# Feed-forward block: weights as the moving operand for gate and up, and 32x32 blocks turned on VectorE

## The chip, the cores and the metric

The kernel runs on one core of a Trainium2 chip. The metric is device time in microseconds (us): the median over three timed executions. Beside them there is one execution recorded by the hardware profiler; all durations below come from that one.

## The reference

A trunk of four pre-norm residual layers on 256 tokens of width 1024, all in float32. Layers 0 and 3 mix tokens with sparse attention (NSA), layer 1 with block attention (MoBA), layer 2 with a short gated convolution. Each layer then applies a dense SwiGLU feed-forward block, and a last RMSNorm ends the trunk. What the change touches is the feed-forward block:

```python
def swiglu(a, w_gate, w_up, w_down):
    return (jax.nn.silu(a @ w_gate) * (a @ w_up)) @ w_down

a = rms_norm(h, norm_ffn[i])                      # h: 256 x 1024
h = h + swiglu(a, ffn_w_gate[i], ffn_w_up[i], ffn_w_down[i])   # D_FF = 2816
```

Per layer that is gate and up, 1024 x 2816 each, and down, 2816 x 1024.

## The kernel before

**Layout.** Activations are kept transposed: features on the 128 partitions, the 256 tokens along the free axis. The residual is eight tiles of 128 x 256 (`self.h`). 2816 features are 22 tiles (`FT`), 1024 are 8 (`KT`).

**Float32 from two parts.** Each operand x is held as a high part (rounded to the type fp32r) and a low part x - high. A product is the sum of three matmuls: high by high, high by low, low by high. Activations are split into a tile of shape [128, 2, 256]: index 0 is high, index 1 is low (`split`, L175: the copy on ScalarE, the subtraction on VectorE).

**Weights.** All weights of the program lie in device memory as one stream of 128x128 tiles in the order of use, cut into parts of 8 tiles (512 KB). `load_part` (L84) issues one transfer of a part from the SP queue into one of 4 `raw` buffers. `split_part` (L91) makes the high part (ScalarE, L109) and the low part (VectorE, L110) into one of 5 `whi` and 5 `wlo` buffers. `take` (L113) hands out tiles in order; when it enters part q it has emitted the load and the split of all parts up to q + 4. A `raw` buffer comes free when its split is done, a `whi`/`wlo` pair when TensorE has used the part. So the transfer of part q + 8 can be issued when part q + 4 is split, and that can be done when TensorE has left part q - 1.

**Matmul.** In `group_wide` (L132) the weight tile is the stationary operand (128x128, loaded ahead of each matmul), and the activations move. With the high weight the high and low activations move as one block of 512 columns and land side by side in one PSUM bank; with the low weight the 256 high activations move:

```python
mm(outs[o], w[0], acts[k].rearrange("p i s -> p (i s)"), ...)   # 512 columns
mm(outs[o][:, :S], w[1], acts[k][:, 0, :], ...)                 # 256 columns
```

That is two matmuls per weight tile, 16 in a part.

**Feed-forward block** (`ffn`, L288). First f = 0 and 1 together (four banks), then one f at a time: eight tiles of gate, eight of up, then `act`. For each f `act` adds the two halves of a bank (`half`: copy on ScalarE L294, add on VectorE L295), scales by the row of reciprocal norms `rb` while f < 7 (L297), applies Silu (L303), multiplies by up (L305), and splits the product into an `ff` tile (L177, L178). From f = 7 on the operand is the normed activation (`normed`, L278), made beside f = 2 to 5. The norm's sums over features (`rms_sums`, L219) are four small matmuls ahead of the last tiles of the first group; `rms_tokens` makes the reciprocal per token (VectorE, GpSimd), `rms_rows` (L234) turns it into rows.

**Down** (`out_proj`, L261) uses `group_wide` with the 22 `ff` tiles: first four output tiles together, feature tile by feature tile (11 parts), then four output tiles one by one.

**Another order that the program already has.** `values` (L338), in the attention layers, has the activations stationary and the weights moving: for each of 8 feature tiles and each half of the tokens, three matmuls of 512 columns, tokens on the partitions of the result:

```python
mm(p, a[:, 0, s], ws[k][0], ...)   # L348
mm(p, a[:, 0, s], ws[k][1], ...)   # L349
mm(p, a[:, 1, s], ws[k][0], ...)   # L350
```

**Order of the work.** The program is written in the order above; a scheduler of the language sets waits and buffers and may interleave what is independent. Every engine and the SP queue then run their own lists in order. PSUM has eight banks, in rings A (4), B (3) and C (1).

Of the kernel before, what the change touches and what calls it, by code (L numbers as in the profile page):

```python
# [10 lines left out]
F32R = mybir.dt.float32r  # L11
AF = mybir.ActivationFunctionType
OP = mybir.AluOpType
# [3 lines left out]
P = 128  # L17
D = 1024
S = 256
KT = D // P  # L20
NT = S // P
DFF = 2816
FT = DFF // P
# [4 lines left out]
PART = 8  # L28
# [2 lines left out]
RAW_BUFS = 4  # L31
W_BUFS = 5
PR_BUFS = 4
FF_BUFS = 24
ROW_BUFS = 7
PT_BUFS = 5
# [15 lines left out]
class Kernel:  # L52
    def __init__(self, ctx, tc, ap):
        self.tc, self.nc, self.ap = tc, tc.nc, ap
        self.const = ctx.enter_context(tc.tile_pool(name="const", bufs=1))
        self.wp = ctx.enter_context(tc.tile_pool(name="wp", bufs=3))
        self.work = ctx.enter_context(tc.tile_pool(name="work", bufs=2))
        self.ps = ctx.enter_context(tc.tile_pool(name="ps", bufs=2, space=PSUM))
        self.pos = 0
        self.raw = {}  # L60
        self.parts = {}
        self.nblk = ap["w"].shape[0]
        self.names = [step for step, name, _, c in stream()
                      for _ in range(len(c) // P * (FT if name == "ffn_w_down" else 4 if step == "F" else KT))][::PART]
        self.n = 0
# [8 lines left out]
    def ff(self, shape, dt=F32R):  # L74
        return self.work.tile(shape, dt, tag="ff", name=self.uid("ff"), bufs=FF_BUFS)

# [7 lines left out]
    def load_part(self, q, cut=1):  # L84
        t = self.wp.tile([P, PART * P], F32, tag="raw", name=f"raw{q}", bufs=RAW_BUFS)
        n = PART * P // cut
        for i in range(cut):
            self.nc.sync.dma_start(t[:, i * n:(i + 1) * n], self.ap["w"][q, :, i * n:(i + 1) * n])
        self.raw[q] = t

    def split_part(self, q):  # L91
# [21 lines left out]
    def take(self, n=1):  # L113

        q, o = divmod(self.pos, PART)
        assert o + n <= PART
        for x in range(q, min(q + AHEAD, self.nblk)):
            if x not in self.parts:
                self.split_part(x)
        self.pos += n  # L120
        hi, lo = self.parts[q]
        return hi[:, o * P:(o + n) * P], lo[:, o * P:(o + n) * P]
# [52 lines left out]
    def split(self, dst, src):  # L175

        self.nc.scalar.copy(dst[:, 0], src)  # L177
        self.nc.vector.tensor_tensor(out=dst[:, 1], in0=src, in1=dst[:, 0].bitcast(F32), op=OP.subtract)  # L178
# [39 lines left out]

    def rms_sums(self):  # L219
        nc = self.nc  # L220
        pt = self.sums = self.bank("C" if self.norm == 8 else "B")
        for t in range(NT):
            c = slice(t * P, (t + 1) * P)
            nc.tensor.matmul(pt[:, t:t + 1], self.ssq[:, c], self.ones, start=True, stop=False)
            nc.tensor.matmul(pt[:, t:t + 1], self.sq[:, c], self.ones, start=False, stop=True)
# [49 lines left out]
            m += n  # L275


    def normed(self, k, norm):  # L278

        nc = self.nc  # L280
        if k % 2 == 0:
            self.pair = self.sb([P, 2, 2, S], "pt", F32R, bufs=PT_BUFS)
        a, x = self.pair[:, k % 2], self.row()
        nc.vector.scalar_tensor_tensor(x, self.h[k], self.gain[:, norm, k:k + 1], self.rb, op0=OP.mult, op1=OP.mult)
        self.split(a, x)
        return a

    def ffn(self, norm):  # L288
        nc = self.nc
        hs, at, final = [], self.begin(norm), []  # L290

        def half(dst, p, scale):

            nc.scalar.copy(dst, p[:, S:])  # L294
            nc.vector.tensor_tensor(out=dst, in0=p[:, :S], in1=dst, op=OP.add)  # L295
            if scale:
                nc.vector.tensor_tensor(out=dst, in0=dst, in1=self.rb, op=OP.mult)  # L297

        def act(pg, pu, scale):
            gu = self.sb([P, 2, S], "gu")  # L300
            sg, hf = self.row(), self.row()
            half(gu[:, 0, :], pg, scale)
            nc.scalar.activation(sg, gu[:, 0, :], AF.Silu)  # L303
            half(gu[:, 1, :], pu, scale)
            nc.vector.tensor_tensor(out=hf, in0=sg, in1=gu[:, 1, :], op=OP.mult)  # L305
            h2 = self.ff([P, 2, S])
            self.split(h2, hf)
            hs.append(h2)

        def products(f, a):  # L310
            p = [self.bank(c) for c in ("AA", "CB", "AA", "AA", "BB")[f - 2 if f < 4 else 2 + f % 3]]
            for o in p:
                self.group_wide([o], a)
            return p

        ps = [self.bank(c) for c in "AABB"]
        self.group_wide(ps, at)
        self.rms_tokens()
        p = products(2, at)
        self.rms_rows()  # L320
        for f in range(2):
            act(ps[2 * f], ps[2 * f + 1], True)
        for f in range(2, FT):
            late = f < 7
            if f > 2:
                p = products(f, at if late else final)
            act(*p, late)
            if len(final) < KT:
                final += [self.normed(len(final) + i, norm) for i in range(2)]
        self.out_proj(hs, norm + 1)  # L330


# [23 lines left out]
    def softmax(self, cols, gates):  # L356

        nc = self.nc
        pr = self.sb([P, 3 * S], "pr", bufs=PR_BUFS)
        mn = self.sb([P, 4], "mn", bufs=3)  # L360
# [496 lines left out]
def wide_tiles(w, cols):  # L857

    k, n = w.shape[0] // P, len(cols) // P
    return w[:, cols].reshape(k, P, n, P).transpose(0, 2, 1, 3).reshape(k * n, P, P)  # L860


def stream():

    r = lambda a, n: np.arange(a, a + n)
    out = lambda w, j, step: [(step, w, j, r(0, 512))] + [(step, w, j, r(m * P, P)) for m in range(4, KT)]
    s = []
    for i in LAYERS:
        j = i // 3
        n = {}  # L870
        if i % 3 == 0:
            for step in NSA_ORDER:
                k = step[0]
                n[k] = m = int(step[1:]) if step[1:] else n.get(k, -1) + 1
                cols = {"A": r(1024, 512), "K": r(1536 + m // 2 * 512 + m % 2 * P, P), "G": r(2480, P),
                        "V": np.concatenate([r(1792, 256), r(2304, 256)]), "q": r(m * P, P)}.get(k)
                if k == "F":
                    s.append((k, "nsa_cmp_w1", j, r(m * 512, 512)))
                elif cols is not None:
                    s.append((k, "nsa_w_in", j, cols))  # L880
            s += out("nsa_w_out", j, "nsa_out")
        elif i % 3 == 1:
            for step in MOBA_ORDER:
                k = step[0]
                n[k] = m = int(step[1:]) if step[1:] else n.get(k, -1) + 1
                cols = {"V": r(2048 + m * 512, 512), "k": r(1024 + m * P, P), "q": r(m * P, P)}.get(k)
                if cols is not None:
                    s.append(("moba_" + k, "moba_w_in", j, cols))
            s += out("moba_w_out", j, "moba_out")
        else:  # L890
            s.append(("conv", "conv_w_in", j, np.concatenate([r(b, P) for b in (1024, 2048, 0)])))
            for c in range(1, KT):
                s += [("conv", "conv_w_in", j, r(b + c * P, P)) for b in (1024, 2048, 0)]
            s += out("conv_w_out", j, "conv_out")
        s.append(("ffn", "ffn_gate_up", i, np.concatenate([r(c, P) for c in (0, DFF, P, DFF + P)])))
        for f in range(2, FT):
            s += [("ffn", "ffn_gate_up", i, r(b + f * P, P)) for b in (0, DFF)]
        s += out("ffn_w_down", i, "down")
    return s


def tiles(x):

    x = dict(x)
    x["ffn_gate_up"] = np.concatenate([x["ffn_w_gate"], x["ffn_w_up"]], axis=2)
    x["nsa_cmp_w1"] = np.concatenate([x["nsa_cmp_k_w1"], x["nsa_cmp_v_w1"]], axis=2)
    ts = []
    for step, name, j, c in stream():
        w = x[name][j]
        ts.append(wide_tiles(w[c], np.arange(512)) if step == "F" else wide_tiles(w, c))  # L910
    t = np.concatenate(ts)
    assert t.shape[0] % PART == 0
    return np.ascontiguousarray(t.reshape(-1, PART, P, P).transpose(0, 2, 1, 3)).reshape(-1, P, PART * P)
# [41 lines left out]
```

## Time and profile before

| | us |
|---|---|
| three timed executions | 1301.71, 1302.19 (median), 1303.94 |
| the profiled execution's own time | 1303.46 |
| its span, first to last instruction | 1301.7 |
| TensorE busy in the span | 1259.3 |
| VectorE busy | 981.8 |
| ScalarE busy | 717.2 |
| GpSimd busy | 309.1 |

The span is 1.76 us shorter than the execution's own time. Busy times of an engine are from start to end of its instructions; a matmul's end is modelled, and matmuls overlap, so the distance between the starts of two matmuls tells what one costs. The mean granted TensorE clock is 0.992 of full speed. DMA moved 215.24 MB.

### The profile page before, as it was taken

The page shows a single profiled execution, that of the slowest core. Times are in us where ns is not written, and L with a number is a line of the kernel's source. Part 1 is how long each engine was busy: PE and PEld are TensorE (multiplying, and loading weights), DVE is VectorE, ACT ScalarE, POOL GpSimd, SP SyncE. Part 2 cuts the span into 40 slices and gives each one's busy share as a digit, 9 for nine tenths or more (in the row PEclk, how much of TensorE's full clock was granted, in tenths as well). Part 3 has the DMA queues.
Part 4 walks back from the last instruction along what each step waited for, and adds up shares of the span by engine and source line. Part 5 has one row for each costly group of instructions (what it writes and reads, how often), then busy time and mean ns, then how long its engine had stood idle before and what let it go on. Part 6 is the DMA issues. An engine that isn't in the chain of part 4 may idle for free.

```text
span 1301.7 us, 21379 instructions
## 1 busy us (share of the span) xinstructions
PE 1259.3 (97%) x7820; PEld 1122.1 (86%) x7820; DVE 981.8 (75%) x1947; ACT 717.2 (55%) x1445; POOL 309.1 (24%) x336
## 2 busy tenths in 40 slices
PE   8888999999998999999999999999998989999997
PEld 8877788888888888888899988888898778888886
DVE  7588799775778888876667789775767797996753
ACT  5469757554335546655434357554324796666532
POOL 2467610000356320000113120000334765000011
PEclk9999999999999999999999999999999999999999
DMA  8623065656554335655555655656555312566551
GB/s 275 234 72 100 33 195 177 196 193 193 181 178 131 108 119 178 211 193 194 168 191 177 194 179 173 200 188 196 182 178 195 98 49 73 187 210 192 186 180 57
DMA packets 60728, 215.24 MB, mean 165 GB/s; under 512 B 7248, under 2 KB 7632, under 8 KB 60624
## 3 DMA queue, kind: packets, MB, share of 16 engines
q1 hardware_dynamic: 60480, 213.85, 50.5%
q8 instruction: 61, 1.00, 0.3%
q14 instruction: 43, 0.35, 0.1%
q10 hardware_dynamic: 144, 0.04, 0.0%
HBM read 212.81 MB, written 1.05 MB: 164 GB/s over the span
## 4 chain that ended last, share of the span: by engine, by line
PE 85%; DVE 8%; ACT 3%; issue 2%; POOL 2%; DMA 1%; POOLq 0%; DVEq 0%; ACTq 0%
PE psA L148 30%; PE psA L152 15%; PE psB L148 11%; PE psB L152 5%; PE psA L128 4%; PE psA L129 4%; PE psA L130 4%; PE psB L560 2%; DVE pt L178 1%; ACT pr L368 1%; DVE ff L178 1%; DVE pr L365 1%; POOL wlo L110 1%; PE psA L348 1%; PE psA L349 1%
## 5 line engine op out<-in xcount | busy, mean ns | idle before, releaser
L109 ACT CAST whi<-raw 128x1024 fp32r<-128x1024 f32 (+1 forms) x356 | 370.2, 1041 | 292.3 <-PE psB L148 110.8
L110 DVE TENSOR_TENSOR wlo<-raw,whi 128x1024 fp32r<-128x1024 f32 (+1 forms) x338 | 413.7, 1229 | 140.0 <-ACT whi L109 134.6
L148 PE MATMUL psA<-ff,whi 128*128 128x512 f32 x840 | 231.3, 396 | 0.2
L148 PEld LDWEIGHTS psA<-ff,whi 128*128 128x128 f32 x840 | 149.0, 188 | 25.0 <-DVE ff L178 0.6
L148 PE MATMUL psA<-pt,whi 128*128 128x512 f32 x640 | 166.4, 395 | 0.0
L206 POOL TENSOR_TENSOR ssq<-ssq,row 128x256 f32<-128x256 f32 x48 | 46.0, 958 | 479.6 <-issue 291.5
L128 PE MATMUL psA<-at,whi 128*128 128x256 f32 x536 | 155.0, 289 | 0.0
L130 PE MATMUL psA<-at,wlo 128*128 128x256 f32 x536 | 154.1, 287 | 0.0
L129 PE MATMUL psA<-at,whi 128*128 128x256 f32 x536 | 154.0, 287 | 0.0
L110 POOL TENSOR_TENSOR wlo<-raw,whi 128x1024 fp32r<-128x1024 f32 x52 | 127.2, 2452 | 83.6 <-ACT whi L109 51.4
L148 PEld LDWEIGHTS psA<-pt,whi 128*128 128x128 f32 x640 | 116.5, 188 | 21.1
L152 PEld LDWEIGHTS psA<-ff,wlo 128*128 128x128 f32 x840 | 122.8, 188 | 12.4
L152 PE MATMUL psA<-ff,wlo 128*128 128x256 f32 x840 | 129.2, 281 | 0.0
L129 PEld LDWEIGHTS psA<-at,whi 128*128 128x128 f32 x536 | 104.8, 196 | 0.5
L128 PEld LDWEIGHTS psA<-at,whi 128*128 128x128 f32 x536 | 104.8, 195 | 0.5 <-DVE row L335 0.2
L130 PEld LDWEIGHTS psA<-at,wlo 128*128 128x128 f32 x536 | 104.7, 195 | 0.0
L152 PEld LDWEIGHTS psA<-pt,wlo 128*128 128x128 f32 x640 | 87.1, 188 | 7.3
L152 PE MATMUL psA<-pt,wlo 128*128 128x256 f32 x640 | 88.9, 281 | 0.0
L148 PE MATMUL psB<-pt,whi 128*128 128x512 f32 x320 | 84.9, 395 | 0.0
L372 POOL TENSOR_SCALAR pr<-pr,rc,gates 128x256 f32<-128x256 f32 (+1 forms) x128 | 70.3, 563 | 40.2 <-DVE rc L370 34.1
L368 ACT ACTIVATE pr<-pr,mn 128x128 f32<-128x128 f32 (+1 forms) x160 | 71.3, 449 | 9.5 <-DVE mn L365 8.7
L303 ACT ACTIVATE row<-gu 128x256 f32<-128x256 f32 x88 | 36.8, 418 | 67.6 <-DVE gu L295 61.2
(216 smaller groups left out, 2215.5 us busy)
## 6 DMA issues: line engine op xcount, KB each, us to landing
raw<-in_w SPq DMA_DIRECT2D x384, 512.0 KB, 4.0
wf<-in_w SPq DMA_DIRECT2D x16, 512.0 KB, 4.7
h<-in_xt SPq DMA_DIRECT2D x4, 256.0 KB, 4.9
raw<-in_w SPq DMA_DIRECT2D x4, 256.0 KB, 5.3
out<-ff SPq DMA_DIRECT2D x4, 256.0 KB, 2.5
w<-in_w SPq DMA_DIRECT2D x2, 256.0 KB, 3.8
mask<-in_mask SPq DMA_DIRECT2D x1, 128.0 KB, 6.8
cneg<-in_cneg SPq DMA_DIRECT2D x1, 128.0 KB, 6.1
```

What stands on the lines that cost most here:

```text
L109: copy(hi[:, c], src[:, c])
L110: eng.tensor_tensor(out=lo[:, c], in0=src[:, c], in1=hi[:, c].bitcast(F32), op=OP.subtract)
L128: mm(out, wt[0], act[0], start=first, stop=False)
L129: mm(out, wt[0], act[1], start=False, stop=False)
L130: mm(out, wt[1], act[0], start=False, stop=last)
L148: mm(outs[o], w[0], acts[k].rearrange("p i s -> p (i s)"), start=(k == 0), stop=(k == n - 1))
L152: mm(outs[o][:, :S], w[1], acts[k][:, 0, :], start=False, stop=False)
L178: self.nc.vector.tensor_tensor(out=dst[:, 1], in0=src, in1=dst[:, 0].bitcast(F32), op=OP.subtract)
L206: (nc.gpsimd if norm else nc.vector).tensor_tensor(out=self.ssq, in0=self.ssq, in1=sq, op=OP.add)
L303: nc.scalar.activation(sg, gu[:, 0, :], AF.Silu)
L368: nc.scalar.activation(pr[:, c], pr[:, c], AF.Exp, bias=mn[:, j:j + 1], scale=-1.0, accum_out=den[:, j:j + 1])
L372: nc.gpsimd.tensor_scalar(pr[:, c], pr[:, c], rc[:, j:j + 1], gates[j], op0=OP.mult, op1=OP.mult)
```

## The change

Gate and up change their operand order: the activations are stationary, the weights move. Features are taken in groups of 4 tiles (five groups, then one of 2). For each of the 8 input tiles a group takes 4 gate and 4 up tiles, one part, and issues for each half of the tokens (t) and for gate and up three matmuls of 512 columns: 12 matmuls in a part. The group of 2 puts gate and up side by side in one bank of 512 columns per t, 6 matmuls per input tile, which is half a part.

The result has tokens on the partitions, so the reciprocal norm is a scalar per partition: Silu on ScalarE reads PSUM with `scale=r`, one VectorE instruction multiplies up by r and by the Silu, and both work on 128 x 512. `rb`, `half`, `act` and `normed` are no longer used here, nor is `rms_rows`.

Down needs features on the partitions. So VectorE transposes the product in 32x32 blocks into `turned`; 16 transfers per group, issued from the SP queue, carry block rows from `turned` to `rows` (each 32 partitions, 128 or 64 numbers for each t, that is 64 pieces of 512 or 256 bytes); then `split` makes the `ff` tiles from `rows`. The order of features in a group is thereby permuted, and the rows of the down weights are permuted on the host to match.

These transfers and splits are jobs that `take` runs when it enters a given part. Four transfers stand right behind the weight load that was issued last, in each of four parts in a row, the first 3 parts after the end of the group; the splits follow 2 parts behind the last of them. `take` looks only at the first job of the list.

`rms_sums` uses ring A for the norms of feed-forward blocks, B otherwise.

```diff
...
+        while self.jobs and self.jobs[0][0] <= q:
+            self.jobs.pop(0)[1]()
...
-        pt = self.sums = self.bank("C" if self.norm == 8 else "B")
+        pt = self.sums = self.bank("C" if self.norm == 8 else "A" if self.norm % 2 else "B")
...
+        nc, at = self.nc, self.begin(norm)
+        mm = nc.tensor.matmul
+        hs = []
+        q = P // 4
+        self.moved = 0
+        def hidden(banks, n):
+            turned = self.sb([P, NT, n * P], "pt", bufs=PT_BUFS)
+            for t, (pg, pu) in enumerate(banks):
+                r = self.rstd[:, t:t + 1]
+                sg, hf = (self.sb([P, n * P], "pr", bufs=PR_BUFS) for _ in range(2))
+                nc.scalar.activation(sg, pg, AF.Silu, scale=r)
+                nc.vector.scalar_tensor_tensor(hf, pu, r, sg, op0=OP.mult, op1=OP.mult)
+                nc.vector.transpose(turned[:, t], hf)
+            rows = self.sb([P, NT, 4, n * q], "pt", bufs=PT_BUFS)
+            dst, ds = [self.ff([P, 2, S]) for _ in range(n)], []
+            hs.extend(dst)
+            def move(i):
+                def job():
+                    with self.tc.issue_after(self.load.ins):
+                        for x in range(i, min(i + MOVES, 16)):
+                            a, b = divmod(x, 4)
+                            nc.sync.dma_start(rows[b * q:(b + 1) * q, :, a],
+                                              turned[a * q:(a + 1) * q, :, b * n * q:(b + 1) * n * q])
+                return job
+            def split():
+                r3 = rows.rearrange("p t a f -> p (t a) f")
+                for c, h2 in enumerate(dst):
+                    self.split(h2.rearrange("p i (a j) -> p i a j", j=q), r3[:, :, c * q:(c + 1) * q])
+            part = max(self.pos // PART + 3, self.moved)
+            for i in range(0, 16, MOVES):
+                self.jobs.append((part, move(i)))
+                part += 1
+            self.moved = part
+            self.jobs.append((part + 2, split))
+        for g in range(0, FT, 4):
+            n = min(4, FT - g)
+            if n == 4:
+                banks = [[self.bank(c) for c in row] for row in (("AA", "AA") if g % 8 else ("BB", "BC"))]
+                outs = banks
+            else:
+                outs = [[self.bank("B")] for _ in range(NT)]
+                banks = [(o[:, :S], o[:, S:]) for o, in outs]
+            for k, a in enumerate(at):
+                if k == KT - 1 and self.sums is None:
+                    self.rms_sums()
+                w = [self.take(4) for _ in outs[0]]
+                for t in range(NT):
+                    s = slice(t * P, (t + 1) * P)
+                    for o, (hi, lo) in zip(outs[t], w):
+                        mm(o, a[:, 0, s], hi, start=(k == 0), stop=False)
+                        mm(o, a[:, 0, s], lo, start=False, stop=False)
+                        mm(o, a[:, 1, s], hi, start=False, stop=(k == KT - 1))
+            if self.rstd is None:
+                self.rms_tokens()
+            hidden(banks, n)
...
-        s.append(("ffn", "ffn_gate_up", i, np.concatenate([r(c, P) for c in (0, DFF, P, DFF + P)])))
-        for f in range(2, FT):
-            s += [("ffn", "ffn_gate_up", i, r(b + f * P, P)) for b in (0, DFF)]
+        for g in range(0, FT, 4):
+            n = min(4, FT - g) * P
+            s.append(("ffn", "ffn_gate_up", i, np.concatenate([r(g * P, n), r(DFF + g * P, n)])))
...
+    rows = [np.arange(g * P, min(g + 4, FT) * P).reshape(4, -1, P // 4).transpose(1, 0, 2).ravel()
+            for g in range(0, FT, 4)]
+    x["ffn_w_down"] = x["ffn_w_down"][:, np.concatenate(rows)]
```

## Rows read from the trace of the kernel before

**Rows 1.** The page: busy time, share of the span and instructions of each engine, and the granted TensorE clock in 40 slices of the span, in tenths.

```profile
PE 1259.3 (97%) x7820; PEld 1122.1 (86%) x7820; DVE 981.8 (75%) x1947; ACT 717.2 (55%) x1445; POOL 309.1 (24%) x336
...
PEclk9999999999999999999999999999999999999999
```

**Rows 2.** The page: the chain of work that ended last, shares of the span by engine and by line and what it writes.

```profile
PE 85%; DVE 8%; ACT 3%; issue 2%; POOL 2%; DMA 1%; POOLq 0%; DVEq 0%; ACTq 0%
PE psA L148 30%; PE psA L152 15%; PE psB L148 11%; PE psB L152 5%; PE psA L128 4%; PE psA L129 4%; PE psA L130 4%; PE psB L560 2%; DVE pt L178 1%; ACT pr L368 1%; DVE ff L178 1%; DVE pr L365 1%; POOL wlo L110 1%; PE psA L348 1%; PE psA L349 1%
```

**Rows 3.** Windows over gate and up in the four layers, from the first matmul that reads `at` to the first one of down: window, its length, busy us and instructions of each engine, then granted clock, busy share of the DMA engines and GB/s.

```profile
171.34:295.82 124.48, 124.48 (x715) 109.07 (x714) 101.28 (x174) 77.51 (x141) 2.55 (x4) 1.00 0.60 195
481.14:605.64 124.50, 124.50 (x715) 109.11 (x714) 100.31 (x172) 77.08 (x140) 4.09 (x4) 1.00 0.58 193
760.07:884.56 124.49, 124.49 (x715) 109.10 (x714) 100.59 (x175) 75.79 (x139) 4.41 (x5) 1.00 0.59 193
1105.39:1229.90 124.51, 124.51 (x716) 109.03 (x715) 101.35 (x175) 77.53 (x141) 2.58 (x4) 1.00 0.60 195
sum 497.98, PE 497.98 PEld 436.31 DVE 403.54 ACT 307.91 POOL 13.64; mean PE 124.50 PEld 109.08 DVE 100.88 ACT 76.98 POOL 3.41
```

**Rows 4.** Timeline of TensorE in gate and up of layer 0: start, length to the modelled end, line, operands, count of matmuls in a run of equal ones.

```profile
230.97 2.02 PE L148 MATMUL psA<-pt,whi 128*128 128x512 f32 x8
232.82 1.10 PE L152 MATMUL psA<-pt,wlo 128*128 128x256 f32 x8
233.77 0.40 PE L148 MATMUL psA<-pt,whi 128*128 128x512 f32 x1
```

**Rows 5.** Timeline of TensorE in `values` of layer 1, the first, a later and the last matmul of one call, and the first one behind it.

```profile
375.40 0.40 PE L348 MATMUL psA<-whi,at 128*128 128x512 f32 x1
...
376.56 0.39 PE L350 MATMUL psA<-whi,at 128*128 128x512 f32 x1
...
386.08 0.39 PE L350 MATMUL psA<-whi,at 128*128 128x512 f32 x1
386.31 0.28 PE L128 MATMUL psA<-at,whi 128*128 128x256 f32 x1
```

**Rows 6.** Timeline of TensorE around the norm's sums and the turned norm in gate and up of layer 0.

```profile
179.72 0.28 PE L224 MATMUL psB<-ones,ssq 128*128 128x1 f32 x2
...
180.53 0.70 PE L148 MATMUL psA<-at,whi 128*128 128x512 f32 x2
...
188.98 0.38 PE L238 MATMUL psB<-ident,rstd 128*128 128x128 f32 x2
189.11 0.48 PE L148 MATMUL psC<-at,whi 128*128 128x512 f32 x1
```

**Rows 7.** Groups of instructions over the whole span: line, engine, operation, out<-in, count, busy us, mean ns of one, idle time before them.

```profile
L110 DVE TENSOR_TENSOR wlo<-raw,whi 128x1024 fp32r<-128x1024 f32 (+1 forms) x338 | 413.7, 1229 | 140.0 <-ACT whi L109 134.6 <-issue 1.5
L109 ACT CAST whi<-raw 128x1024 fp32r<-128x1024 f32 (+1 forms) x356 | 370.2, 1041 | 292.3 <-PE psB L148 110.8 <-PE psA L148 102.5 <-PE psA L129 24.6
...
L178 DVE TENSOR_TENSOR ff<-row,ff 128x256 fp32r<-128x256 f32 x120 | 60.4, 504 | 5.0 <-ACT ff L177 4.5
...
L177 ACT CAST ff<-row 128x256 fp32r<-128x256 f32 x120 | 48.9, 407 | 33.2 <-DVE row L773 15.8 <-DVE row L335 14.9 <-DVE row L305 1.8
...
L178 DVE TENSOR_TENSOR pt<-psB,pt 128x512 fp32r<-128x512 f32 x64 | 40.0, 651 | 4.0 <-ACT pt L177 3.4
...
L303 ACT ACTIVATE row<-gu 128x256 f32<-128x256 f32 x88 | 36.8, 418 | 67.6 <-DVE gu L295 61.2 <-DVE gu L297 6.2
...
L177 ACT CAST pt<-psB 128x512 fp32r<-128x512 f32 x64 | 32.9, 562 | 6.5 <-PE psB L703 4.5 <-PE psB L444 1.1 <-PE psB L445 0.4
...
L284 DVE SCALAR_TENSOR_TENSOR row<-h,gain,rb 128x256 f32<-128x256 f32 x32 | 14.0, 481 | 0.0
...
L232 POOL TENSOR_TENSOR rstd<-var,mhalf 128x2 f32<-128x2 f32 x9 | 8.2, 908 | 59.0 <-DVE var L230 59.0
```

**Rows 8.** The view of DMA: the queue of the weights (packets, MB, share of 16 engines), and issues with count, KB each and median us from issue to landing.

```profile
q1 hardware_dynamic: 60480, 213.85, 50.5%
...
raw<-in_w SPq DMA_DIRECT2D x384, 512.0 KB, 4.0
...
out<-ff SPq DMA_DIRECT2D x4, 256.0 KB, 2.5
```

**Rows 9.** Timeline of the SP queue in gate and up of layer 0, one issue of a weight load: start, length.

```profile
239.35 0.33 SPq L88 DMA_DIRECT2D raw<-in_w  x1
```

**Rows 10.** Timeline of all engines in down of layer 0, two parts: where a part's first matmul starts, and where the cast and the subtraction of a later part start.

```profile
301.43 0.86 PE L148 MATMUL psA<-ff,whi 128*128 128x512 f32 x3
...
303.54 1.05 ACT L109 CAST whi<-raw 128x1024 fp32r<-128x1024 f32 x1 [1.76 <-PE psB L148]
...
304.25 0.85 PE L148 MATMUL psA<-ff,whi 128*128 128x512 f32 x3
...
304.63 1.23 DVE L110 TENSOR_TENSOR wlo<-raw,whi 128x1024 fp32r<-128x1024 f32 x1 [1.59 <-ACT whi L109]
```

More of the change, by code (lines that the diff above doesn't have):

```diff
@@ L33 @@
 PR_BUFS = 4
+MOVES = 4
 FF_BUFS = 24
@@ L61, in __init__ @@
         self.parts = {}
+        self.jobs = []
         self.nblk = ap["w"].shape[0]
@@ L87, in load_part @@
         for i in range(cut):
-            self.nc.sync.dma_start(t[:, i * n:(i + 1) * n], self.ap["w"][q, :, i * n:(i + 1) * n])
+            self.load = self.nc.sync.dma_start(t[:, i * n:(i + 1) * n], self.ap["w"][q, :, i * n:(i + 1) * n])
         self.raw[q] = t
@@ L275, in out_proj @@
             m += n
[L278 to L286, printed above, removed]
-    def ffn(self, norm):
[L289 to L322, printed above, removed]
-        for f in range(2, FT):
[L324 to L329, printed above, removed]
@@ L894, in stream @@
             s += out("conv_w_out", j, "conv_out")
-        s.append(("ffn", "ffn_gate_up", i, np.concatenate([r(c, P) for c in (0, DFF, P, DFF + P)])))
-        for f in range(2, FT):
-            s += [("ffn", "ffn_gate_up", i, r(b + f * P, P)) for b in (0, DFF)]
+        for g in range(0, FT, 4):
+            n = min(4, FT - g) * P
+            s.append(("ffn", "ffn_gate_up", i, np.concatenate([r(g * P, n), r(DFF + g * P, n)])))
         s += out("ffn_w_down", i, "down")
```

## Prediction

> **What bounds the kernel now.** I read four views, in this order. The page's busy shares come first [rows 1]: TensorE is busy 97% of the span and its clock stands at 2.4 GHz in every slice, so only what shortens or delays TensorE's list can move the time. The chain of waits says the same [rows 2]: 85% of the chain is TensorE, and the two lines of `group_wide`, L148 and L152, are its first four entries. Then the windows over gate and up [rows 3]: 124.48 + 124.50 + 124.49 + 124.51 = 497.98 us in four layers, TensorE busy in all of it. There is no wait to remove there; VectorE is busy 403.54 and ScalarE 307.91 us of it, neither is the bound, and their work that the change drops is worth nothing by itself. Last come the timelines, for the distance between matmul starts.
>
> In gate and up as they are, 8 matmuls of 512 columns take 232.82 - 230.97 = 1.85 us and the 8 of 256 behind them 233.77 - 232.82 = 0.95 [rows 4]. A part of 8 weight tiles thus costs 2.80 to 2.81 us; 22 x 2 x 8 = 352 tiles are 44 parts a layer, 44 x 2.81 = 123.6, and the norm's sums (180.53 - 179.72 = 0.81) and the turned norm (189.11 - 188.98 = 0.13) [rows 6] make it 124.5, as the windows have it. So one matmul of 512 costs 231 to 232 ns and one of 256 costs 119; 512 columns at 2.4 GHz are 213.3 ns, 256 are 106.7. Each matmul carries 12 to 19 ns on top of its columns.
>
> **The matmuls.** Before, a part streams 8 x 512 + 8 x 256 = 6144 columns in 16 matmuls; after, 12 x 512 = 6144 in 12. What changes is the time on top. The trace has the new form already: `values` runs `at` as the stationary side and `whi`, `wlo` as the moving one, 8 x 2 x 3 = 48 matmuls between 375.40 and 386.31 [rows 5], (386.31 - 375.40)/48 = 227.3 ns each, waits for weights included. The first five take 232 ((376.56 - 375.40)/5), the 42 between 376.56 and 386.08 226.7. I take 227.3: 12 x 227.3 = 2.728 us for a part, against 2.81. A layer has 44 x 12 = 528 matmuls, 528 x 0.2273 = 120.0, and with the sums, which stay at 0.81, 120.8; four layers 483.3. Gain: 498.0 - 483.3 = 14.7 us, the turned norm's 0.13 a layer in it. The ends for this term: 226.7 throughout gives 16.0, 232 throughout gives 44 x (2.81 - 2.784) + 0.13 = 1.3 a layer, 5.1.
>
> One rule of the Trainium skill speaks against this gain. The rows give 13.4 to 14 ns above the columns for a matmul of 512 in the new form. The page TensorE: Matmul & The Clock Gate, section Back-to-back issue gap, says that a warm matmul costs its columns at 2.4 GHz plus about 2.5 ns; four matmuls fewer in a part would then be worth 10 ns, 176 parts 1.8 us. The trace does not agree with that size, before or after; the rule's case is rival 2.
>
> **ScalarE and VectorE.** For a group of 4 (8 parts, 8 x 2.73 = 21.8 us of TensorE) ScalarE has 8 weight casts of 1.041, two Silu of 128x512 and four casts of 0.407 [rows 7]. A Silu of 256 costs 0.418 and a copy of 512 from PSUM 0.562, so one of 512 lies between 0.56 and 2 x 0.418 = 0.84; I take 0.65. Sum 8.3 + 1.3 + 1.6 = 11.2. VectorE has 8 subtractions of 1.229, two products of 512 (0.651 for a two-input operation on 512 from PSUM, 2 x 0.481 as the upper end; I take 0.7), two transposes of 512 and four subtractions of 0.504. The trace shows no 32x32 transpose; from below it is a pass over 256 elements (0.42 to 0.5), from above four passes over 512 (2.6); I take 0.65, a pass over 512. Sum 9.8 + 1.4 + 1.3 + 2.0 = 14.5, with the upper ends 18.9. Both stay under 21.8. They cost nothing, since a part is split four parts ahead of its use, 10.9 us, while a cast and a subtraction take 2.3 and a whole group's `hidden` at most 6 in front of them.
>
> **Banks.** Groups alternate between BBBC and AAAA, so a bank has 21.8 us to be read. The exception is the sixth group: its two B banks are those of gate and up of the first token half of the fifth, released without such a pause. That half ends 6 x 0.227 = 1.36 us before the group does (time T). Silu from T - 1.2 to T - 0.5 frees the first, the product from about T - 0.3 to T + 0.4 the second; TensorE wants them at T and, three matmuls later, at T + 0.7. No wait, with 0.3 us to spare; if a weight cast (1.04) stands in front, about 1 us a layer. Ring A for the sums takes nothing: the sums are read at once, 2.7 us ahead of the next group.
>
> **The transfers on SP.** One issue occupies SP for 0.33 us [rows 9], so a part with four of them has 5 x 0.33 = 1.6 of 2.73 us. The first four stand behind the load of part base + 7 (base is the first part after the group), which leaves at about T - 0.3, when part base + 3 is split. They wait for the last transpose: Silu, product and transpose of the second half end near T + 2.3, with the upper ends T + 6. Behind them waits the load of base + 8, which before could go once part base + 4 is split, at about T + 3.4. Held until T + 7.6 at worst, it lands 4.0 us later [rows 8] and is split in 2.3, by T + 14; TensorE wants it at T + 21.8. In the sixth group the list's first job is the fifth's split at base + 5, so twelve transfers go out there together, 4 us of SP, and four at base + 6; the same slack covers that.
>
> **The packets.** Weights are 60480 packets in 50.5% of 16 x 1301.7 us, 0.174 us each at 213.85 MB / 60480 = 3.5 KB [rows 8]. A group of 4 adds 16 x 64 = 1024 packets of 512 B. By bytes one costs 0.174/7 = 0.025, the group 1.6 us of 21.8 on the 16 engines, with a share of 0.60 in the stage [rows 3]: nothing. The other end, a price per packet, is rival 3.
>
> **The end of the block.** Down wants the sixth group's first tile at its part 10 (tile 80 of 88). Its last transfers follow the load of part base + 10, near the end of part 2, and have landed in part 4 or 5. Its split is a job of part 9, behind the cast and subtraction of part 13. In down a cast starts 0.71 us before a part's first matmul (303.54 against 304.25) and the subtraction 0.38 after it (304.63) [rows 10]; the subtraction ends at 0.38 + 1.23 = 1.6, the two tiles' own 0.5 each at 2.6, the part ends at 2.82. It just fits; late by up to 0.5 in some layers.
>
> **The sum.** I set 1.0 us for the two tight places over four layers: net 14.7 - 1.0 = 13.7. The profiled execution took 1303.46 us, 1.76 more than its span; 1303.46 - 13.7 = 1289.8. It lies 1.27 above the median of the runs, 1302.19, so for a median 1288.5.
>
> **The rivals.**
> 1. The matmul of 512 keeps its 232 ns. For it: L148 has the same columns and the same number of stationary loads per matmul; the first five of `values` take 232 too. Against it: the other 42 run at 226.7, and gate and up have 528 in a row, broken only by the sums. Gain 5.1 less 1.0: 1298.
> 2. The columns alone set the price, and the same 6144 cost the same: at most the turned norm's 0.5 us is won, 1301 to 1302. The cited rule comes close to it, with 1.8 us, 1300.4. For it only that columns are equal; against it the 119 ns of a matmul of 256, twice which is more than one of 512.
> 3. Slower: a packet of the new transfers costs as much as one of the weights, and the 16 DMA engines become the bound of gate and up. In the stage a part's 128 packets take 0.60 x 2.81 x 16 = 27 us of engines, 0.21 each. A layer has 44 x 128 = 5632 packets of weights and would get 6 x 1024 = 6144 more: 11776 x 0.21 / 16 = 154.6 us against the 123.6 of before, four layers 124 us slower, 1426. It is slower than before from 0.129 us a packet on ((123.6 x 16 - 5632 x 0.21)/6144). For it: 32 partitions and two small pieces each, a shape that the trace has nowhere. Against it: the price by bytes, 0.025, is a fifth of that.
>
> **Chances.** The forecast, with all that the tight places may cost, 0.84 (its own range 1286 to 1293); rival 1 0.06, rival 2 0.03, rival 3 0.07. The range 1285.5 to 1298 takes in the upper gain of 16.0 without any wait (1286.2) and rival 1. A measurement of this kernel can tell about 0.2%, 2.6 us, from no change. Faster by more: the forecast and rival 1, 0.90; within it: rival 2, 0.03; slower: 0.07.
>
> **What would show it.** Right: windows over gate and up of about 121 us, TensorE busy in all of it, matmul starts 227 ns apart, no matmul of the sixth group waiting for ScalarE or VectorE, none of down for `ff`. Rival 1: 232 apart and no waits. Rival 3: a DMA share near 1 and casts waiting for `raw`. The forecast is wrong if TensorE waits more than about 0.5 us a group for weights, or if 512 columns cost more with banks changing every three matmuls than in `values`, where they don't.

## The result, and the profile after

The changed kernel takes 1287.16 us (median of four, 1285.36 to 1289.81) against 1301.95 us in the same sitting: a ratio of 0.9885, 95% interval 0.9864 to 0.9906. Run again later beside other kernels it took 1285.96 us, ratio 0.9879 (0.9865 to 0.9894). The forecast was 1288.5 us. The profiled execution took 1286.44 us, 17.0 less than the one of before.

The page: busy time of each engine, and the queue of the weights and the blocks.

```profile
PE 1242.1 (97%) x7108; PEld 1084.0 (84%) x7108; DVE 900.1 (70%) x1655; ACT 654.2 (51%) x1197; POOL 307.4 (24%) x336
...
q1 hardware_dynamic: 91200, 225.41, 56.7%
```

TensorE has 712 matmuls fewer and is as full as before; VectorE and ScalarE lost 82 and 63 us of work. The windows over gate and up, cut as in [rows 3], tell where the time went:

```profile
171.54:292.22 120.68, 120.68 (x538) 99.99 (x536) 78.27 (x94) 60.51 (x75) 2.56 (x4) 1.00 0.69 215
477.04:597.70 120.66, 120.66 (x538) 100.00 (x536) 77.35 (x92) 59.77 (x74) 3.08 (x3) 1.00 0.70 213
752.12:872.78 120.66, 120.66 (x537) 99.99 (x536) 77.51 (x92) 58.82 (x73) 3.34 (x4) 1.00 0.71 212
1092.04:1212.71 120.67, 120.67 (x537) 100.00 (x536) 78.29 (x94) 60.59 (x75) 2.56 (x4) 1.00 0.70 215
sum 482.67, PE 482.67 PEld 399.98 DVE 311.42 ACT 239.69 POOL 11.54; mean PE 120.67 PEld 99.99 DVE 77.86 ACT 59.92 POOL 2.88
```

497.98 - 482.67 = 15.3 us are gained here, and TensorE is busy in all of it. The longest waits of TensorE are those of the attention layers and of the start, as before; no line of gate and up or of `group_wide` stands in the list:

```profile
PE psB L542 <- DVE row L353: 6.7, 2, 3.4
PE psA L174 <- ACT whi L111: 5.7, 1, 5.7
```

The other 1.9 us of the span (1301.7 - 1284.5 = 17.2) lie in the attention layers, and I don't ascribe them to the change: the stretch of layer 3 ahead of its feed-forward block took 157.50 us at a granted clock of 1.00 in this profile and 159.92 at 0.97 in the second profile of the same kernel, against 159.04 at 0.98 before. The first window below is of the kernel before, the second of the changed kernel's first profile, the third of its repetition; the number behind the busy times is the granted clock.

```profile
946.35:1105.39 159.04, 149.07 (x1029) 134.58 (x1028) 122.29 (x344) 100.80 (x272) 89.04 (x98) 0.98 0.35 117
```

```profile
934.54:1092.04 157.50, 146.41 (x1029) 131.92 (x1028) 122.28 (x344) 100.85 (x273) 89.23 (x98) 1.00 0.38 118
```

```profile
931.78:1091.70 159.92, 150.13 (x1030) 135.76 (x1028) 122.37 (x344) 100.96 (x272) 89.24 (x98) 0.97 0.37 116
```

The timeline of TensorE in gate and up: 17 matmuls from the start of the first row to the start of the last, 3.85/17 = 226.5 ns each.

```profile
268.42 0.39 PE L342 MATMUL psB<-whi,at 128*128 128x512 f32 x1
268.64 0.39 PE L343 MATMUL psB<-wlo,at 128*128 128x512 f32 x1
...
272.27 0.39 PE L344 MATMUL psB<-whi,at 128*128 128x512 f32 x1
```

The new operations, from the views of their lines (ns, shortest/median/longest; first and last start), and the issues of DMA:

```profile
L299 ACT ACTIVATE pr<-psA,rstd x16: 675/684/692, 215.3 to 1179.6; 128x512 f32<-128x512 f32 x16
...
L300 DVE SCALAR_TENSOR_TENSOR pr<-psA,rstd,pr x16: 739/744/746, 216.6 to 1180.8; 128x512 f32<-128x512 f32 x16
...
L301 DVE STREAM_TRANSPOSE pt<-pr x48: 445/672/712, 195.3 to 1214.1; 128x512 f32<-128x512 f32 x40, 128x256 f32<-128x256 f32 x8
...
L311 SPq DMA_DIRECT2D pt<-pt x384: 585/595/1540, 198.6 to 1229.7; - x192
```

```profile
raw<-in_w SPq DMA_DIRECT2D x384, 512.0 KB, 4.3
pt<-pt SPq DMA_DIRECT2D x320, 32.0 KB, 3.0
```

Silu 0.68, product 0.74, transpose 0.67 us: close to the 0.65, 0.7 and 0.65 taken. But one transfer's issue holds SP for 0.6 us, not 0.33.

### The profile page after: what moved, and what is told of

Its sections match the earlier page's. It is cut to its first block, busy times and chain, and to the rows that moved or that the text cites. A ratio compares the mean times of both kernels' runs of the same rounds, so it can differ in the third digit from the quotient of the medians.

```text
span 1284.5 us, 19976 instructions
## 1 busy us (share of the span) xinstructions
PE 1242.1 (97%) x7108; PEld 1084.0 (84%) x7108; DVE 900.1 (70%) x1655; ACT 654.2 (51%) x1197; POOL 307.4 (24%) x336
## 4 chain that ended last, share of the span: by engine, by line
PE 84%; DVE 8%; ACT 3%; issue 2%; POOL 2%; DMA 1%; POOLq 0%; DVEq 0%; ACTq 0%
PE psA L152 15%; PE psA L156 7%; PE psB L342 6%; PE psB L344 6%; PE psB L343 6%; PE psA L344 5%; PE psA L343 5%; PE psA L342 5%; PE psA L132 4%; PE psA L133 4%; PE psA L134 4%; PE psB L152 2%; PE psB L578 2%; PE psC L344 2%; PE psC L343 2%
## 5 line engine op out<-in xcount | busy, mean ns | idle before, releaser
L342 PE MATMUL psB<-whi,at 128*128 128x512 f32 x352 | 137.4, 390 | 0.0
L344 PE MATMUL psB<-whi,at 128*128 128x512 f32 x352 | 137.0, 389 | 0.0
L343 PE MATMUL psB<-wlo,at 128*128 128x512 f32 x352 | 137.0, 389 | 0.0
L156 PEld LDWEIGHTS psA<-ff,wlo 128*128 128x128 f32 x840 | 122.8, 188 | 12.4
L342 PE MATMUL psA<-whi,at 128*128 128x512 f32 x256 | 99.6, 389 | 0.0
L343 PE MATMUL psA<-wlo,at 128*128 128x512 f32 x256 | 99.6, 389 | 0.0
L344 PE MATMUL psA<-whi,at 128*128 128x512 f32 x256 | 99.6, 389 | 0.0
L344 PEld LDWEIGHTS psB<-whi,at 128*128 128x128 f32 x352 | 66.1, 188 | 13.8
```

The lines of the kernel that those rows point to most:

```text
L156: mm(outs[o][:, :S], w[1], acts[k][:, 0, :], start=False, stop=False)
L342: mm(o, a[:, 0, s], hi, start=(k == 0), stop=False)
L343: mm(o, a[:, 0, s], lo, start=False, stop=False)
L344: mm(o, a[:, 1, s], hi, start=False, stop=(k == KT - 1))
```

## The experiments

**The yardstick.** The changed kernel again.

> The changed kernel once more, beside the other kernels of this group, as their yardstick. Expected 1287 us, as measured before; the windows over gate and up 120.7 us in each layer again. The attention layers may differ by 1 to 2 us from the first profile of it, since their mean granted clock differed between the two profiles (0.98 before, 1.00 after in layer 3).

1285.96 us, gate and up 120.66 to 120.68 us. As said above, the stretch of layer 3 differed by 2.4 us from the first profile. Differences of one or two microseconds are therefore read from windows of the stage, not from the totals.

**Halves.**

```diff
-mm(o, a[:, 0, s], hi, start=(k == 0), stop=False)
+halves = (slice(0, S), slice(S, 2 * S))
+for c in halves if k else (slice(0, 2 * S),):
+    mm(o[:, c], a[:, 0, s], hi[:, c], start=(k == 0), stop=False)
...
```

(and the other two matmuls alike, each as two halves)

> The changed kernel with each matmul of 512 columns in gate and up issued as two of 256 (the first of each group of sums stays whole): the same 6144 columns a part in 24 matmuls instead of 12. Theory (each matmul carries about 13 ns on top of its columns, so the number of matmuls sets the gain): 24 x 119.9 ns = 2.878 us a part instead of 2.722; 5.5 x (7 x 2.878 + 2.825) + 0.81 = 127.2 us a layer against 120.7, four layers 26 us: 1313 us. Rival (columns alone set the price): 120.7 us a layer, 1287 us.

1312.03 us, ratio 1.0088 (1.0069 to 1.0107), slower than the kernel before. The window of layer 0:

```profile
172.84:300.26 127.42, 127.42 (x1043) 126.41 (x1042) 78.93 (x95) 60.75 (x75) 2.57 (x4) 1.00 0.65 205
```

506 matmuls more in a layer (1034 instead of 528) cost 127.42 - 120.68 = 6.74 us, 13.3 ns each, at the same columns. The columns alone don't set the price. Each half also loads its stationary operand anew: weight loads fill 126.41 us of the window, against 99.99 in the changed kernel. Whether the 13.3 ns are the price of a matmul or of its weight load is not separated here.

**The old mix, weights moving.**

```diff
-mm(o, a[:, 0, s], lo, start=False, stop=False)
+for c in (slice(0, S), slice(S, 2 * S)):
+    mm(o[:, c], a[:, 0, s], lo[:, c], start=False, stop=False)
```

> The changed kernel where of the three matmuls the middle one (low weights) is issued as two of 256 columns: a part has 8 matmuls of 512 and 8 of 256, just the mix of the kernel before, but with weights moving. It tells why a matmul of 512 costs 232 ns in the kernel before and 227 here. Theory A (its neighbours: next to matmuls of 256 it costs 232, in a row of its own kind 227): 8 x 232 + 8 x 119 = 2.808 us a part, 124.4 us a layer, about 1302 us. Theory B (its operands: weights moving cost 227 whatever stands beside): 8 x 226.8 + 8 x 119.9 = 2.773 us a part, 122.8 us a layer, about 1296 us.

1296.04 us, ratio 0.9949 (0.9933 to 0.9966). The total is that of theory B, but the window is 123.56 us, between its 122.8 and the 124.4 of theory A. Window and timeline:

```profile
171.54:295.10 123.56, 123.56 (x714) 108.01 (x713) 78.33 (x95) 60.15 (x75) 2.54 (x4) 1.00 0.67 211
```

```profile
230.29 0.40 PE L342 MATMUL psC<-whi,at 128*128 128x512 f32 x1
230.53 0.39 PE L344 MATMUL psC<-wlo,at 128*128 128x256 f32 x2
230.76 0.40 PE L345 MATMUL psC<-whi,at 128*128 128x512 f32 x1
230.99 0.39 PE L342 MATMUL psB<-whi,at 128*128 128x512 f32 x1
```

Beside 256s the successor of a 512 starts after 230 to 240 ns, but the two 256s take 230 together, 115 each and not 119. Some time goes over from one size to the other. (123.56 - 0.81)/44 = 2.79 us a part, where 8 x 226.8 + 8 x 119.9 would be 2.773: 2 ns more for each pair of a 512 and a 256. This kernel has the matmul counts of before with the operands exchanged, so it divides the gain of a layer, 124.50 - 120.67 = 3.83 us: 0.13 is the turned norm, 124.37 - 123.56 = 0.8 the exchange of operands together with another order of the sizes (before, eight 512s and then eight 256s; here one 512, two 256s, one 512), 123.56 - 120.67 = 2.9 that eight matmuls of 256 become four of 512. What the exchange is worth without the other order this run doesn't tell.

**What makes 232.** Three kernels change down and the output projection, where weights are stationary and activations move.

```diff
-mm(outs[o][:, :S], w[1], acts[k][:, 0, :], start=False, stop=False)
+mm(outs[o], w[1], acts[k].rearrange("p i s -> p (i s)"), start=False, stop=False)
```

> The changed kernel where in down and in the mixers' output projection the low weights also meet the high and the low activations (one more product, low by low): 960 tiles have two matmuls of 512 columns instead of one of 512 and one of 256, activations still moving. Theory A (neighbours: in a row of 512s each costs 227): 960 x (0.4536 - 0.351) = 98 us more, 1385 us, matmul starts 227 ns apart. Theory B (operands: activations moving cost 232): 960 x (0.464 - 0.351) = 108 us more, 1395 us, starts 232 apart.

1394.22 us, starts 232 ns apart (eight matmuls from 310.83 to 312.69): theory B, neighbours of 256 are not needed for 232.

```profile
310.83 0.86 PE L152 MATMUL psA<-ff,whi 128*128 128x512 f32 x3
...
312.69 0.87 PE L156 MATMUL psA<-ff,wlo 128*128 128x512 f32 x3
```

Then both operands from one side; in the diff of the second, `part` is the pair of weight buffers that the tile comes from.

```diff
-mm(outs[o], w[0], acts[k].rearrange("p i s -> p (i s)"), ...)
+mm(outs[o], acts[k][:, 0, :P], acts[k].rearrange("p i s -> p (i s)"), ...)
```

> The changed kernel where down and the mixers' output projection run two matmuls of 512 columns per tile with activations on both sides, stationary and moving (what they compute is not the product; the weights are loaded and split but not used there). With weights stationary and activations moving the same two cost 232 ns each. Theory A (the stationary weights are the reason for 232): starts 227 ns apart. Theory B (the moving activations are): 232 apart.

```diff
-mm(outs[o], w[0], acts[k].rearrange("p i s -> p (i s)"), ...)
+mm(outs[o], w[0], part[0][:, 4 * P:], ...)
```

> The counterpart: in down and the output projection both sides are weights, the tile stationary as before and the second half of the same part moving, 512 columns, twice per tile (again not the product). Theory A (the stationary weights are the reason for 232): starts 232 ns apart. Theory B (the moving activations are): 227 apart.

Activations on both sides: eight matmuls from 310.77 to 312.58, 226 ns each. Weights on both sides: from 311.33 to 313.14, 226 too. Each ran once, in 1405.63 and 1386.04 us. The first total is longer than the 1394.22 of the kernel above though its matmuls are shorter; I use the distances of starts alone and don't explain that total.

```profile
310.77 0.84 PE L152 MATMUL psA<-ff 128*128 128x512 f32 x3
...
312.58 0.84 PE L157 MATMUL psA<-ff 128*128 128x512 f32 x3
```

```profile
311.33 0.84 PE L157 MATMUL psA<-wlo 128*128 128x512 f32 x3
...
313.14 0.84 PE L153 MATMUL psA<-whi 128*128 128x512 f32 x3
```

Both theories are contradicted: neither stationary weights nor moving activations cost 232 by themselves. Only the two together do, and each kernel changed the addresses of an operand as well as its kind. The cause of these 5 ns stays open.

**No transfers.**

```diff
-rows = self.sb([P, NT, 4, n * q], "pt", bufs=PT_BUFS)
+rows = turned.rearrange("p t (a f) -> p t a f", a=4)
...
-nc.sync.dma_start(rows[b * q:(b + 1) * q, :, a], ...)
```

> The changed kernel without the transfers: the splits read the turned blocks where VectorE left them, so the features of down are in the wrong place, while every other instruction stays. Theory (the transfers are hidden entirely): within 0.2% of the changed kernel, 1287 us, gate and up 120.7 us a layer. Rival (the SP queue, 0.64 us from one of these issues to the next, costs something that the four windows do not show): faster by 2 us or more, below 1285.

1285.43 us, ratio 0.9875 (0.9858 to 0.9891); its window in layer 0 is 120.68 us, that of the changed kernel to the hundredth. The 384 transfers are hidden entirely. Not for nothing: casts wait 77.7 us in all for weights in the repeated profile of the changed kernel, 22.8 without the transfers. That is slack being used up where TensorE doesn't see it. The two rows, the changed kernel (repeated) first:

```profile
ACT whi L111 <- DMA raw<-in_w: 77.7, 54, 5.4
```

```profile
ACT whi L111 <- DMA raw<-in_w: 22.8, 17, 3.9
```

**Twice the transfers.**

```diff
+again = self.sb([P, NT, 4, n * q], "pt", bufs=PT_BUFS)
...
+nc.sync.dma_start(again[b * q:(b + 1) * q, :, a], turned[...])
```

> The changed kernel with every transfer of the blocks issued twice, the second time into a buffer that nothing reads: 32 transfers a group. Theory (SP is the resource that comes next): in the four parts that carry them SP needs 4 x (8 x 0.64 + 0.53) = 22.6 of 10.9 us, falls 11.7 behind and wins 9.6 back in the four parts without; a load has some 12.8 us of slack, so from the second or third group on TensorE waits for weights, 1 to 10 us a layer: 1291 to 1327 us. Rival (SP's time is free as long as the 16 DMA engines are below full): 1287 us, TensorE busy in all of gate and up.

1473.79 us, ratio 1.1322 (1.1303 to 1.1342). Right in kind, far off in size: the expectation went up to 1327. The DMA engines are busy 0.62 of the stage, less than the 0.69 of the changed kernel, but casts wait 436.9 us for weights, up to 14.1 at a time, and TensorE, which now pauses for 14.9 us of gate and up, has a granted clock of 0.95 there instead of 1.00:

```profile
ACT whi L111 <- DMA raw<-in_w: 436.9, 194, 14.1
```

```profile
168.98:317.46 148.48, 133.63 (x538) 102.62 (x537) 77.75 (x93) 59.05 (x74) 2.55 (x4) 0.95 0.62 182
317.46:399.16 81.70, 66.53 (x354) 57.28 (x352) 45.24 (x61) 28.35 (x37) 10.40 (x8) 0.90 0.58 175
```

The first row is gate and up of layer 0, the second down. The list of SP for one group:

```profile
225.07 0.59 SPq L312 DMA_DIRECT2D pt<-pt  x1
...
247.50 7.69 SPq L90 DMA_DIRECT2D raw<-in_w  x5
255.25 0.59 SPq L312 DMA_DIRECT2D pt<-pt  x1
```

Its 32 transfers and the three loads between them take 22.4 us without a pause, the five loads behind them, one of which waits until a `raw` buffer comes free, 7.7: 30.2 us, where the group's matmuls need 21.8. So the list of SP is what comes next. My figure let the queue catch up between groups; instead gate and up of layer 0 grew by 27.8 us, and down, where I had expected none of it, by 19.9 (81.70 against 61.76 in the changed kernel).

**All sixteen at once.**

```diff
-MOVES = 4
+MOVES = 16
...
-self.jobs.append((part + 2, split))
+self.jobs.append((part, split))
```

> The changed kernel with all 16 transfers of a group behind one weight load, and the splits one part later instead of three parts behind the last transfer. Theory (the slack is wide): SP is held for 16 x 0.64 = 10.2 us, the load of part base + 8 leaves at about T + 12.6, lands at T + 16.9 and is split by T + 19.2, where TensorE wants it at T + 21.8; splits that wait for the landing hold casts up by about 5 us, which the four parts of lead (10.9 us) cover. So 1287 us. Rival (the stagger and the later splits are what makes the change work): TensorE waits for weights once a group, 1 us or more each, 24 groups: 1311 us or more, with casts waiting for raw or splits waiting for transfers in front of it.

1325.39 us, ratio 1.0187 (1.0166 to 1.0207): the rival. The waits of ScalarE and of the weight loads of TensorE:

```profile
ACT ff L181 <- DMA pt<-pt: 145.1, 24, 9.5
```

```profile
PEld psB L342 <- ACT pr L299: 24.3, 4, 6.5
```

Its timelines of ScalarE and of SP around the end of the fifth group:

```profile
268.27 1.06 ACT L111 CAST whi<-raw 128x1024 fp32r<-128x1024 f32 x1 [0.48 <-DMA raw<-in_w]
278.85 1.33 ACT L181 CAST ff<-pt 128x256 fp32r<-128x256 f32 x4 [9.52 <-DMA pt<-pt]
...
286.83 1.26 ACT L299 ACTIVATE pr<-psB,rstd 128x512 f32<-128x512 f32 x2
```

```profile
266.39 10.94 SPq L311 DMA_DIRECT2D pt<-pt  x16
```

SP needs 10.9 us for sixteen issues, here those of the fourth group. ScalarE, in order, stands 9.5 us ahead of their split until they have landed, makes up four casts, and reaches the fifth group's Silu late. The sixth group wants just those banks: 24.3 us of TensorE in four layers, 6.1 a layer. That is the tight place of the prediction, where I had reckoned with a Silu at T - 1.2, and two thirds of the 9.4 us by which gate and up grew in layer 0 (130.07 us against 120.68).

Which of the two edits did it?

```diff
-MOVES = 4
+MOVES = 16
...
-self.jobs.append((part + 2, split))
+self.jobs.append((part + 5, split))
```

> All 16 transfers of a group behind one weight load as in the slow kernel with both edits (1325 us), but the splits at the part where the changed kernel has them (9 parts after the group's end). Theory A (the early splits were the price: ScalarE, in order, stood 6 to 9 us a group in the split until the transfers had landed, and the Silu of the fifth group came late for the sixth group's banks): no wait of ScalarE for the transfers, gate and up back at 120.7 us a layer, 1286 us. Theory B (the weight loads behind 16 issues, 10.9 us of SP, were the price): still 1310 us or more, casts waiting for raw.

1323.3 us, ratio 1.0153 (1.0137 to 1.017), and the same row:

```profile
ACT ff L181 <- DMA pt<-pt: 139.5, 24, 9.2
```

By the expectation that would be theory B. By the row it isn't: ScalarE still waits for the transfers, since the split still stands there, behind four casts of the group (269.87 is the start of the fourth, 279.69 that of the split) and not behind seven as in the changed kernel. With the splits given out at part 4 and at part 9 behind the group, the list of ScalarE has them in the same place: the scheduler orders that list, and the part named in the source did not decide it. So the edit didn't reach the list of ScalarE, and the run doesn't separate the two theories. The other half:

```diff
-self.jobs.append((part + 2, split))
+self.jobs.append((part, split))
```

> The changed kernel with only the splits moved: right behind the fourth part's transfers (7 parts after the group's end) instead of two parts later. The transfers of a group are issued from T + 2.5 to T + 14.6 in the changed kernel and land 3 us later, T + 17.6; ScalarE reaches the split at part base + 7, T + 19. Theory A: it just fits, 1286 to 1290 us, with some waits of ScalarE or VectorE for the transfers of about 1 us. Theory B (two parts of slack were needed): gate and up above 122 us a layer, 1291 us or more.

1284.47 us, ratio 0.9858 (0.9839 to 0.9877): no loss, theory A's outcome; TensorE waits once, 0.6 us in the last layer, for a Silu ahead of the sixth group. Here too the split stands behind the seventh cast of the group, as in the changed kernel. Of the edits "four behind each of four loads" and "splits parts later" the first makes the difference. Whether through the loads or through the place of the split that comes with it stays open.

**Two sums less.** A version that the new order makes room for.

```diff
-if k < KT - 1:
+if k < KT - 1 or norm % 2:
     (nc.gpsimd if norm else nc.vector).tensor_tensor(out=self.ssq, in0=self.ssq, in1=sq, op=OP.add)
...
-nc.tensor.matmul(pt[:, t:t + 1], self.ssq[:, c], self.ones, start=True, stop=False)
-nc.tensor.matmul(pt[:, t:t + 1], self.sq[:, c], self.ones, start=False, stop=True)
+whole = self.norm % 2 == 1
+nc.tensor.matmul(pt[:, t:t + 1], self.ssq[:, c], self.ones, start=True, stop=whole)
+if not whole:
+    nc.tensor.matmul(pt[:, t:t + 1], self.sq[:, c], self.ones, start=False, stop=True)
```

> The changed kernel with two matmuls fewer in the norm's sums of the feed-forward blocks: GpSimd adds the eighth square too, which it has time for, since the sums now stand 7 parts (19 us) into the first group instead of 8 us. Two matmuls of 0.2 us less in each of four layers: gate and up 120.3 instead of 120.7 us a layer, about 1.6 us less in all, 1284.5 us. Rival (GpSimd is late with the eighth add): TensorE waits ahead of the sums, no gain.

1283.5 us, ratio 0.985 (0.9835 to 0.9865): the lowest median, though its interval overlaps that of the kernel with the early splits. The windows over gate and up give

```profile
sum 480.85, PE 480.85 PEld 398.26 DVE 313.04 ACT 239.42 POOL 16.51; mean PE 120.21 PEld 99.56 DVE 78.26 ACT 59.85 POOL 4.13
```

482.67 - 480.85 = 1.8 us, and TensorE is busy in all of it, so GpSimd's eighth add is not late; the rest of its distance to the changed kernel is within what the attention layers vary by.

## Why the prediction was right

**The matmuls.** Forecast 120.8 us a layer at 227.3 ns, measured 120.67, that is (120.67 - 0.81)/528 = 227.0 in the mean and 226.5 in the row shown: the row of `values` was the right one to carry over, and its mean with the first five in it was a little too high. "At 2.4 GHz in every slice" was read too roughly: a 9 stands for 0.9 or more. The granted clock is 1.00 over gate and up [rows 3], but 0.98 over the stretch of layer 3 shown above. Rival 1 (232 ns stays) and rival 2 (columns alone) fell in the changed kernel's own windows, rival 2 once more in the halves. The rule of the Trainium skill, TensorE: Matmul & The Clock Gate, Back-to-back issue gap, of about 2.5 ns over the columns, would by estimate make the halves 506 x 2.5 ns = 1.3 us a layer slower; the trace shows 6.74 us. The section gives that rule for the isolated gap and not for a stream in which weights are loaded too, a condition that the prediction leaves out. The measurement decides: in this kernel, where every matmul has its own weight load, a matmul more costs 13.3 ns.

**ScalarE and VectorE.** The durations were within 0.05 us of those taken, and nothing of them reached TensorE.

**The tight places.** I had set 1.0 us for the sixth group's banks and for the last splits; no matmul waited in either. The profiled execution came 3.4 us under my 1289.8: this 1.0, 15.3 - 14.7 = 0.6 of the matmuls, and the 1.9 of the attention layers, 3.5 together. That the banks are tight indeed is shown by the two kernels with sixteen transfers at once.

**The transfers on SP.** Here a term was mis-sized: "One issue occupies SP for 0.33 us" was read from the weight load. A timeline of the SP queue of the changed kernel shows

```profile
203.90 0.53 SPq L90 DMA_DIRECT2D raw<-in_w  x1
204.47 2.52 SPq L311 DMA_DIRECT2D pt<-pt  x4
207.09 0.53 SPq L90 DMA_DIRECT2D raw<-in_w  x1
```

A load and four transfers take 207.09 - 203.90 = 3.2 us, more than the 2.73 of a part, not the 1.6 I had reckoned. It cost nothing because only four parts in eight carry them, and a load has some eight microseconds of slack (split by T + 14 at worst by the prediction, wanted at T + 21.8). Spread over four parts the queue falls 2 us behind; the expectation that sixteen in one go were harmless was built on slack for loads and overlooked the engine that waits in order for the transfers.

**The packets.** The queue has 30720 new packets: 24576 pieces and 384 x 16 = 6144 of 4 bytes, 16 for each transfer. By the trace's records of single packets one of 512 bytes takes 0.034 us, one of 256 bytes 0.021, one of 4 bytes 0.009: somewhat over the 0.025 by bytes and far under the 0.129 of rival 3. The rise of the queue's share would give (0.567 x 1284.5 - 0.505 x 1301.7) x 16 / 30720 = 0.037 each, but that puts down to them also that a weight packet of 4096 bytes took 0.206 us instead of 0.200.

**The end of the block.** I took the splits to stand in part base + 9, 24.5 us after the group; that is three parts behind the last transfers, not the two that the section on the change says. The list of ScalarE in the changed kernel, from the second Silu of the fourth group on:

```profile
259.10 0.69 ACT L299 ACTIVATE pr<-psA,rstd 128x512 f32<-128x512 f32 x1 [0.40 <-PE psA L344]
...
276.10 1.05 ACT L111 CAST whi<-raw 128x1024 fp32r<-128x1024 f32 x1 [1.67 <-PE psC L344]
277.05 1.32 ACT L181 CAST ff<-pt 128x256 fp32r<-128x256 f32 x4
```

The split comes 18 us after the group, more than two parts sooner than I took it. The sixth group, the one that the reckoning was for, ends at 292.22. Its last transfers and its split, from the timelines of SP and of ScalarE:

```profile
297.43 9.46 SPq L311 DMA_DIRECT2D pt<-pt  x12
...
307.57 2.51 SPq L311 DMA_DIRECT2D pt<-pt  x4
```

```profile
311.27 1.05 ACT L111 CAST whi<-raw 128x1024 fp32r<-128x1024 f32 x1 [4.70 <-DMA raw<-in_w]
312.22 0.71 ACT L181 CAST ff<-pt 128x256 fp32r<-128x256 f32 x2
```

The twelve transfers in one go hold SP for 9.5 us, not 4, and the last four go out in part 5 of down, not near the end of part 2; a cast then waits 4.7 us for weights. But the split starts 20 us after the group, 8 us ahead of part 10, which wants it. It fitted by the place that the scheduler gave the split, not by the reckoning, and so by luck.

## What to carry to other kernels

Where TensorE is full, count matmuls and not only columns: the same 6144 columns, weights moving, cost 2.79 us as 8 + 8 and 2.72 as 12, and 2.88 if nearly all are of 256. Price a stage that the trace has elsewhere by that row, mean over the whole call. And before small transfers are put on the queue that feeds the weights, find what one issue of that shape costs there, and look which engine, working in order, waits for their landing; where a scheduler orders the lists, read its order before believing a place written in the source.

## What was not expected of the hardware

An issue of a transfer of 64 pieces, SBUF to SBUF, holds the SP queue for 0.60 us, one of a weight load of 128 rows for 0.33, and for 0.53 right behind such transfers. In a row of its own kind a matmul of 512 columns costs 232 ns with weights stationary and activations moving and 227 with the two exchanged or with both from the same side; why is open.
